# Sixteen instead of eight expert blocks between the query heads, with the low halves of their weights made on GpSimd

## The chip, the cores and the metric

The kernel runs on one core of one Trainium2 chip. The metric is the device time of one execution in microseconds (us), lower being better. The core has TensorE for matmuls, VectorE, ScalarE and GpSimd for work on tiles in SBUF, SyncE as a queue that starts transfers, and 16 DMA engines. The profile calls the engines PE, DVE, ACT, POOL and SP; PEld is TensorE's loading of weights.

## The reference

Two layers act on 512 tokens of width 1024. Each has a mixer (a gated linear recurrence in layer 0, attention in layer 1) and then a feed-forward part with 16384 experts, of which each token uses 16 in each of 8 heads. The change lies in that second part:

```python
def retrieve_chunk(xc):
    q = (xc @ q_w).reshape(TOKEN_CHUNK, PEER_HEADS, 2, PEER_HALF)
    s1 = jnp.einsum('thd,hnd->thn', q[:, :, 0], subkey1)
    s2 = jnp.einsum('thd,hnd->thn', q[:, :, 1], subkey2)
    v1, i1 = lax.top_k(s1, PEER_TOPK)
    v2, i2 = lax.top_k(s2, PEER_TOPK)
    cand = (v1[..., :, None] + v2[..., None, :]).reshape(...)
    top_s, top_c = lax.top_k(cand, PEER_TOPK)
    e1 = jnp.take_along_axis(i1, top_c // PEER_TOPK, axis=-1)
    e2 = jnp.take_along_axis(i2, top_c % PEER_TOPK, axis=-1)
    expert = e1 * PEER_KEYS + e2
    g = jax.nn.softmax(top_s, axis=-1)
    u = jnp.take(expert_u, expert, axis=0)
    act = jax.nn.gelu(jnp.einsum('thkd,td->thk', u, xc))
    w = g * act
    return jnp.einsum('thk,thkd->td', w, jnp.take(expert_v, expert, axis=0))
```

## The kernel before

Three of the four tiles of 128 tokens (384 tokens) are computed densely: each of 128 blocks of 128 experts is projected for all of them (the matrix `expert_u`), the result goes through the GELU, is multiplied by a gate that is zero where the expert wasn't chosen, and is multiplied by the block of `expert_v`. The fourth tile is gathered: GpSimd fetches the chosen rows of `expert_u` and `expert_v` by indirect transfers (L700), 128 of each, and VectorE reduces them (L706, L716).

A product of two float32 numbers is made of three matmuls. `split` (L189) has ScalarE copy a tile to a shorter format, the high half (`whi`), and VectorE subtract that from the tile, the low half (`wlo`, L192). All weights pass through one `Stream`, in the order of a plan written out by hand: `fill` (L129) loads a pair of blocks with SyncE into `wraw` (two buffers) and splits each block into `whi` and `wlo` (four buffers each), and `take` (L144) keeps three blocks ahead.

The expert part of a layer has three stages. In the query stage `queries` (L530) goes over 8 heads: two projections of queries of 512 columns (`proj_t`, L254, or `proj_early`, L235, for the first), the split of each query into `qh` and `ql`, scores against 128 keys in `sps` (L545 to L547), and the 16 best of each token by VectorE (`top16`, L521). After every second head (`ups_after`, L485), `first_up` (L554) projects two blocks of experts ahead, eight in all (`NEARLY`), and puts their activations into DRAM (`ascr`, L558). In the routing stage 48 more blocks are projected ahead (up to `NFIRST`, 56), and beside each of them a `Background` runs as much of the routes and gates as the credit `GP` pays. In the value stage (from `expert_in`, L745) the 72 blocks that were not projected ahead come first, each projected on the spot (L751); then the 56 whose activations are loaded again (L753). TensorE multiplies each by its block of `expert_v` (18 matmuls of 512 columns, L769). Beside each block `pump` pays credit for the gathered tile: 4.6 for the first eight blocks, then `PUMP[0]`, 3.7, and `PUMP[1]`, 1.4, for those from DRAM; one row costs 1.2 (fetch and reduction), and the route of the tile 18.5 in all. When the gathered tile is done, credit that is left pays for nothing, or, in layer 0, for some of the next mixer's modulation (`after`).

The code is recorded and then ordered for each engine by a scheduler, so that an engine's queue need not follow the text; in each queue instructions run in order. GpSimd's queue held, around this stage, four small operations of the norm, 48 memsets for the routes' tables (L566 to L568), and the row fetches of the value stage.

Of the kernel before, what the change touches and what calls it, by code (L numbers as in the profile page):

```python
# [26 lines left out]
PH = 8  # L27
# [3 lines left out]
ROWO = [sum(ROWN[:i]) for i in range(TOPK)]  # L31
NCAND = sum(ROWN)
NEG = -3.0e38
NFIRST = 56
NEARLY = 8
PUMP = (3.7, 1.4)
GP = 4.0
GSCALE = 32768.0
M0 = 12
# [10 lines left out]
def pool(tc, **kw):  # L50
    return tc.tile_pool(reuse_waits="tile", **kw)
# [67 lines left out]
class Stream:  # L119
# [3 lines left out]
    def __init__(self, g, items, ahead=3):  # L123
        self.g, self.ahead = g, ahead
        self.blocks = [(i, b) for i in items for b in range(i[2])]
        self.raw, self.parts = None, []
        self.n = 0

    def fill(self, last):  # L129

        g, nc = self.g, self.g.nc
        last = min(last, len(self.blocks) - 1)
        while len(self.parts) <= last:
            (src, shape, n), b = self.blocks[len(self.parts)]
            if b == 0:
                self.raw = g.wraw.tile([128, n, *shape], F32, name="wraw", tag="wraw")
                nc.sync.dma_start(self.raw, src)
            raw = self.raw[:, b]
            hi = g.wsp.tile([128, *shape], F32R, name="whi", tag="whi")
            lo = g.wsp.tile([128, *shape], F32R, name="wlo", tag="wlo")  # L140
            split(g, hi, lo, raw)
            self.parts.append((hi, lo))

    def take(self, ahead=None):  # L144
# [42 lines left out]
        g.nc.scalar.activation(out[:, half * 512:(half + 1) * 512], ps, AF.Copy)  # L187


def split(g, hi, lo, raw):  # L190
    g.nc.scalar.activation(hi, raw, AF.Copy)  # L191
    g.nc.vector.tensor_sub(lo, raw, hi)  # L192


def norm(g, cols, ng, mod=None):
# [41 lines left out]
def proj_early(g, psum, h, m):  # L237

    nc = g.nc
    w = [g.stream.take(0) for _ in range(m)]  # L240
    hhi, hlo = h
    ps = [psum.tile([128, S], F32, name="pacc", tag="acc") for _ in range(m)]
    for s in range(KD):
        for b in range(min(s + 1, m)):
            for k in range(s + 1) if s == b else (s,):
                nc.tensor.matmul(ps[b], w[b][0][:, k, :], hhi[:, k, :], start=(k == 0), stop=False)
                nc.tensor.matmul(ps[b], w[b][0][:, k, :], hlo[:, k, :], start=False, stop=False)
                nc.tensor.matmul(ps[b], w[b][1][:, k, :], hhi[:, k, :], start=False, stop=(k == KD - 1))
    return ps


def proj_t(g, psum, h, n=S):

    nc = g.nc  # L254
    whi, wlo = g.stream.take()
    hhi, hlo = h
    ps = psum.tile([128, S], F32, name="pacc", tag="acc")[:, :n]
    for k in range(KD):
        nc.tensor.matmul(ps, whi[:, k, :], hhi[:, k, :n], start=(k == 0), stop=False)  # L259
        nc.tensor.matmul(ps, whi[:, k, :], hlo[:, k, :n], start=False, stop=False)  # L260
        nc.tensor.matmul(ps, wlo[:, k, :], hhi[:, k, :n], start=False, stop=(k == KD - 1))  # L261
    return ps
# [221 lines left out]

def ups_after(hd):  # L485

    n = 2 * NEARLY // PH
    return range(hd // 2 * n, hd // 2 * n + n) if hd % 2 else range(0)


def peer_plan(q_w, sk, uT, v):

    plan = []
    up = [(uT[c], (KD, 128), 2) for c in range(PK // 2)]
    for hd in range(PH):
        q = (q_w[hd], (KD, 128), 2)
        plan += [(sk[hd], (2, 128), 1), q] if hd else [q, (sk[hd], (2, 128), 1)]
        plan += up[ups_after(hd).start // 2:ups_after(hd).stop // 2]
    down = [(v[2 * c:2 * c + 2].rearrange("c p a b -> p c a b"), (2, 512), 2) for c in range(PK // 2)]
    n = NFIRST // 2  # L500
    plan += up[NEARLY // 2:n]
    for c in range(n, PK // 2):
        plan += [up[c], down[c]]
    return plan + down[:n]


def peer(g, h, u, v, grow_fn, after, nd):


    tc, nc = g.tc, g.nc  # L510
# [3 lines left out]
    gscr = g.dram.tile([NB, 128, 128, 16], F32, name="gscr", tag="gscr")  # L514
    ascr = g.dram.tile([NFIRST, 128, ND], F32, name="ascr", tag="ascr")
    with pool(tc, name="pk", bufs=1) as pk:
# [5 lines left out]
        def top16(val, idx, src, n):  # L522
            tk = pk.tile([128, 128], F32, name="tk", tag="tk", bufs=4)
            V.max(val[:, 0:8], src)
            V.max_index(idx[:, 0:8], val[:, 0:8], src)
            V.match_replace(tk[:, :n], val[:, 0:8], src, NEG)
            V.max(val[:, 8:16], tk[:, :n])
            V.max_index(idx[:, 8:16], val[:, 8:16], tk[:, :n])

        def queries(pw, psum):  # L530

            early = []
            for hd in range(PH):
                if hd == 0:
                    early = proj_early(g, psum, h, 2)
                skh, skl = g.stream.take()
                for w in range(2):
                    ps = early.pop(0) if early else proj_t(g, psum, h)
                    qh = pw.tile([128, S], F32R, name="qh", tag="qh")
                    ql = pw.tile([128, S], F32R, name="ql", tag="ql")  # L540
                    split(g, qh, ql, ps)
                    sps = psum.tile([128, TC, 128], F32, name="sps", tag="sps", bufs=4)
                    for t in range(TC):
                        ts = slice(t * 128, (t + 1) * 128)
                        T.matmul(sps[:, t, :], qh[:, ts], skh[:, w, :], start=True, stop=False)  # L545
                        T.matmul(sps[:, t, :], qh[:, ts], skl[:, w, :], start=False, stop=False)
                        T.matmul(sps[:, t, :], ql[:, ts], skh[:, w, :], start=False, stop=True)  # L547
                    for t in range(TC):
                        top16(vals[w][:, t, hd, :], idxs[w][:, t, hd, :], sps[:, t, :], 128)
                for c in ups_after(hd):  # L550
                    first_up(pw, psum, c)

        def first_up(pw, psum, c):

            ps = proj_t(g, psum, h, ND)
            at = pw.tile([128, ND], F32, name="at", tag="at")
            A.activation(at, ps, AF.Gelu)
            nc.scalar.dma_start(ascr[c], at)  # L558
# [168 lines left out]
        with pool(tc, name="pu", bufs=1) as pu, pool(tc, name="pw", bufs=2) as pw, \  # L727
# [4 lines left out]
            bg = Background(*[route(t) for t in range(nd)], *[dense_gates(t, pu, pw, psum) for t in range(nd)])  # L732
            for c in range(NEARLY, NFIRST):
                first_up(pw, psum, c)
                bg.pump(GP)
            bg.finish()
        with pool(tc, name="vw", bufs=2) as vw, pool(tc, name="vps", bufs=1, space=PSUM) as psum:
# [4 lines left out]
            acc = [[psum.tile([128, 512], F32, name=f"vacc{t}{d}") for d in range(2)] for t in range(nd)]  # L742
            order = [*range(NFIRST, PK), *range(NFIRST)]
            ready = {}

            def expert_in(i):

                c = order[i]
                at = vw.tile([128, ND], F32, name="at2", tag="at2", bufs=3)
                if c >= NFIRST:  # L750
                    A.activation(at, proj_t(g, psum, h, ND), AF.Gelu)  # L751
# [20 lines left out]
            def pump(i):  # L772
                bg.pump(4.6 if i < 8 else PUMP[0] if order[i] >= NFIRST else PUMP[1])

# [386 lines left out]
```

## Time and profile before

| | us |
|---|---|
| runs timed | 3399.68, 3401.50, 3401.56 (median 3401.5) |
| profiled execution | 3391.94 |
| its span, from first to last instruction | 3390.2 |
| TensorE, VectorE, ScalarE, GpSimd busy | 3158.9, 2647.0, 1482.6, 790.7 |
| mean granted clock of TensorE | 0.973 |

The stages are cut from the timeline. In layer 0 the query stage runs from 314 us (the first projection) to 465 us (the last score), the routing stage to 751 us, the first part of the value stage to 1380 us and the rest to about 1648 us, where the gathered rows end at about 1578 us. In layer 1 the cuts are at 2040, 2199, 2485, 3112 and 3385 us. In the tables of windows each engine's busy time stands with the number of instructions in brackets, and a matmul's time reaches from its start to its modelled end, so that neighbouring matmuls overlap; the step from one start to the next tells more.

### The profile page before, as it was taken

Reading aid. Unit: us, or ns where it says so; the run is one execution under the profiler, and the core shown is the slowest. Engines: PE = TensorE matmul, PEld = TensorE weight load, DVE = VectorE, ACT = ScalarE, POOL = GpSimd, SP = SyncE. Lnnn points to the kernel's source line nnn. Section 1 sums busy time; section 2 is a strip of 40 time slices with the busy share of each in tenths; the row PEclk is TensorE's granted clock in tenths of the full one; section 3 lists DMA queues with packets and bytes.
Section 4 is the critical chain, followed back from the end, with each engine's and each line's share of the span. In section 5 each row is a group of like instructions: output and inputs, shape, how many; then the busy total and the mean of one; then the engine's idle time right before and its main releaser. Section 6 shows DMA issues by size and latency. Waiting matters only on the chain.

```text
span 3390.2 us, 44187 instructions
## 1 busy us (share of the span) xinstructions
PE 3158.9 (93%) x16256; PEld 2712.4 (80%) x16256; DVE 2647.0 (78%) x5245; ACT 1482.6 (44%) x2065; POOL 790.7 (23%) x672
## 2 busy tenths in 40 slices
PE   5987999999999999999999989999999999999999
PEld 4875889988888888777777767889988888887777
DVE  7867889876777787877679777799867777788775
ACT  4872237863333333333458723257843333332332
POOL 0000000003544454441000000000025454444430
PEclk9998999999999999999999989999999999999999
DMA  6445235778888889988441152336879888899994
GB/s 255 149 146 178 103 126 197 257 273 288 315 299 315 322 322 329 351 310 324 141 153 58 49 192 92 114 133 245 283 250 323 320 302 314 321 330 331 325 335 169
DMA packets 300762, 816.91 MB, mean 241 GB/s; under 512 B 24320, under 2 KB 153344, under 8 KB 272000
## 3 DMA queue, kind: packets, MB, share of 16 engines
q1 hardware_dynamic: 197312, 453.85, 38.6%
q0 software_dynamic: 75008, 269.00, 21.8%
q10 hardware_dynamic: 28224, 91.24, 6.9%
q8 instruction: 127, 2.08, 0.2%
q14 instruction: 91, 0.75, 0.1%
HBM read 733.00 MB, written 81.00 MB: 240 GB/s over the span
## 4 chain that ended last, share of the span: by engine, by line
issue 23%; PE 23%; DVE 19%; DMA 17%; POOL 10%; ACT 7%; SPq 0%; ACTq 0%; POOLq 0%; DVEq 0%
POOL rows L700 10%; DMA at<-ascr 6%; DMA rows<-in_l_v_dram,ei 6%; PE pacc L259 4%; DVE wlo L192 4%; PE pacc L260 4%; PE pacc L261 4%; PE vacc L769 2%; DVE accg L716 2%; PE gps L683 2%; DMA mw<-in_l_ffn_mw_dram 2%; DMA mw<-in_l_mix_mw_dram 1%; DVE mw L160 1%; ACT st L685 1%; ACT whi L191 1%
## 5 line engine op out<-in xcount | busy, mean ns | idle before, releaser
L191 ACT ACTIVATE whi<-wraw 128x1024 fp32r<-128x1024 f32 (+2 forms) x646 | 663.1, 1035 | 740.2 <-PE pacc L260 314.4
L261 PE MATMUL pacc<-hhi,wlo 128*128 128x384 f32 (+1 forms) x2632 | 935.4, 355 | 39.9 <-DVE wlo L192 39.9
L259 PE MATMUL pacc<-hhi,whi 128*128 128x384 f32 (+1 forms) x2632 | 930.6, 354 | 15.9 <-ACT at L751 14.4
L260 PE MATMUL pacc<-hlo,whi 128*128 128x384 f32 (+1 forms) x2632 | 930.0, 353 | 0.0
L192 DVE TENSOR_TENSOR wlo<-wraw,whi 128x1024 fp32r<-128x1024 f32 (+2 forms) x646 | 767.7, 1194 | 171.8 <-ACT whi L191 169.5
L769 PE MATMUL vacc<-whi,wh 128*128 128x512 f32 x1536 | 613.8, 400 | 23.6 <-ACT wh L191 23.4
L700 POOL DMA_INDIRECT rows<-in_l_u_dram,ei x256 | 370.1, 1446 | 1127.5 <-DMA wraw<-in_l_uT_dram 716.7
L769 PE MATMUL vacc<-wlo,wh 128*128 128x512 f32 x1536 | 612.9, 399 | 20.7 <-DVE wlo L192 20.5
L769 PE MATMUL vacc<-whi,wl 128*128 128x512 f32 x1536 | 612.1, 399 | 5.7 <-DVE wl L192 5.5
L261 PEld LDWEIGHTS pacc<-hhi,wlo 128*128 128x128 f32 x2632 | 502.7, 191 | 71.2 <-DVE wlo L192 49.8
L259 PEld LDWEIGHTS pacc<-hhi,whi 128*128 128x128 f32 x2632 | 503.1, 191 | 49.4 <-ACT at L751 16.6
L260 PEld LDWEIGHTS pacc<-hlo,whi 128*128 128x128 f32 x2632 | 502.2, 191 | 29.2 <-issue 2.4
L191 ACT ACTIVATE wh<-at 128x384 fp32r<-128x384 f32 x256 | 133.8, 524 | 806.4 <-DVE at L757 789.3
L700 POOL DMA_INDIRECT rows<-in_l_v_dram,ei x256 | 377.2, 1474 | 454.6 <-DVE accg L716 396.9
L706 DVE SCALAR_TENSOR_TENSOR rows<-rows,hn 128x1024 f32<-128x1024 f32 x256 | 304.6, 1221 | 130.3 <-DMA rows<-in_l_u_dram,ei 130.1
L769 PEld LDWEIGHTS vacc<-wlo,wh 128*128 128x128 f32 x1536 | 290.4, 189 | 94.6 <-DVE wlo L192 30.9
L769 PEld LDWEIGHTS vacc<-whi,wh 128*128 128x128 f32 x1536 | 290.7, 189 | 93.7 <-ACT wh L191 30.9
L769 PEld LDWEIGHTS vacc<-whi,wl 128*128 128x128 f32 x1536 | 290.7, 189 | 85.3 <-DVE wl L192 16.3
L716 DVE SCALAR_TENSOR_TENSOR accg<-rows,act,accg 128x1024 f32<-128x1024 f32 x254 | 325.5, 1282 | 41.0 <-DMA rows<-in_l_v_dram,ei 38.4
L757 DVE TENSOR_TENSOR at<-at,gtile 128x384 f32<-128x384 f32 x256 | 140.6, 553 | 108.4 <-DMA at<-ascr 105.9
L685 ACT ACTIVATE st<-gps 128x512 f32<-128x512 f32 x192 | 185.3, 1117 | 47.6 <-PE gps L683 45.2
L192 DVE TENSOR_TENSOR wl<-at,wh 128x384 fp32r<-128x384 f32 x256 | 141.3, 554 | 68.8 <-ACT wh L191 68.8
(266 smaller groups left out, 3229.5 us busy)
## 6 DMA issues: line engine op xcount, KB each, us to landing
wraw<-in_l_uT_dram SPq DMA_DIRECT2D x128, 1024.0 KB, 6.4
wraw<-in_l_v_dram SPq DMA_DIRECT2D x128, 1024.0 KB, 8.4
gscr<-st ACTq DMA_DIRECT2D x48, 1024.0 KB, 5.6
gtile<-gscr SPq DMA_DIRECT2D x32, 1536.0 KB, 12.3
mw<-in_l_mix_mw_dram SPq DMA_DIRECT2D x48, 512.0 KB, 6.4
mw<-in_l_ffn_mw_dram SPq DMA_DIRECT2D x48, 512.0 KB, 4.0
ascr<-at ACTq DMA_DIRECT2D x112, 192.0 KB, 4.1
at<-ascr SPq DMA_DIRECT2D x112, 192.0 KB, 5.2
```

The costliest lines, as they stand in the source:

```text
L191: g.nc.scalar.activation(hi, raw, AF.Copy)
L192: g.nc.vector.tensor_sub(lo, raw, hi)
L259: nc.tensor.matmul(ps, whi[:, k, :], hhi[:, k, :n], start=(k == 0), stop=False)
L260: nc.tensor.matmul(ps, whi[:, k, :], hlo[:, k, :n], start=False, stop=False)
L261: nc.tensor.matmul(ps, wlo[:, k, :], hhi[:, k, :n], start=False, stop=(k == KD - 1))
L683: T.matmul(gps[:, r, :], p2[:, tk_, :, :].rearrange("p a b -> p (a b)"), pg[i][:, :, tk_, :], start=(i == 0), stop=(i == 1))
L685: A.activation(st[:, :, q * 4:q * 4 + 4].rearrange("p e t -> p t e"), gps, AF.Copy, scale=1.0 / GSCALE)
L700: nc.gpsimd.indirect_dma_start(out=rows, out_offset=None, in_=src, in_offset=bass.IndirectOffsetOnAxis(ap=ei[:, j:j + 1], axis=0))
L706: V.scalar_tensor_tensor(r, r, 1.0, hn, op0=OP.mult, op1=OP.mult, accum_out=act[:, j:j + 1]))
L716: tc.keep_in_program_order(V.scalar_tensor_tensor(acc, r, w, acc, op0=OP.mult, op1=OP.add))
L757: V.tensor_tensor(at.rearrange("p (b t) -> p b t", t=16), at.rearrange("p (b t) -> p b t", t=16), env["gt"][:, :, c % 8, :], op=OP.mult)
L769: T.matmul(acc[t][d], x[:, ts], y[:, d, :], start=(i == 0 and x is wh and y is vh), stop=(i == PK - 1 and x is wl))
```

## The change

`NEARLY` goes from 8 to 16 and `NFIRST` from 56 to 64, so the routing stage still has 48 blocks and the value stage projects 64 on the spot and loads 64. `ups_after` gives two blocks after each head. While `queries` is recorded, the stream's subtractions go to GpSimd. `PUMP[1]` goes from 1.4 to 1.55.

```diff
-NFIRST = 56
-NEARLY = 8
-PUMP = (3.7, 1.4)
+NFIRST = 64
+NEARLY = 16
+PUMP = (3.7, 1.55)
...
+        self.on_pool = False
...
-            split(g, hi, lo, raw)
+            split(g, hi, lo, raw, nc.gpsimd if self.on_pool else nc.vector)
...
-def split(g, hi, lo, raw):
+def split(g, hi, lo, raw, eng=None):
     g.nc.scalar.activation(hi, raw, AF.Copy)
-    g.nc.vector.tensor_sub(lo, raw, hi)
+    (eng or g.nc.vector).tensor_sub(lo, raw, hi)
...
 def ups_after(hd):
-    n = 2 * NEARLY // PH
-    return range(hd // 2 * n, hd // 2 * n + n) if hd % 2 else range(0)
+    n = NEARLY // PH
+    return range(hd * n, hd * n + n)
...
             early = []
+            g.stream.on_pool = True
             for hd in range(PH):
...
                     first_up(pw, psum, c)
+            g.stream.on_pool = False
```

GpSimd's queue in layer 0, from the last memsets of the tables (`thr`, `rowlen`, `col`) to the row fetches, before:

```order
55 L566 MEMSET thr 128x64
56 L567 MEMSET rowlen 128x64
57 L568 MEMSET col 128x64
58 L94 IOTA ji 128x128
59 L700 DMA rows<-in_l_u_dram,ei 128x1024 x128
60 L700 DMA rows<-in_l_v_dram,ei 128x1024 x128
```

In the changed kernel the low halves of the weights follow the memsets (the narrow ones are those of the keys):

```order
58 L570 MEMSET rowlen 128x64
59 L571 MEMSET col 128x64
60 L193 TENSOR_TENSOR wlo<-wraw,whi 128x1024
61 L193 TENSOR_TENSOR wlo<-wraw,whi 128x256
62 L193 TENSOR_TENSOR wlo<-wraw,whi 128x1024 x4
```

That pattern of four wide and one narrow goes on for the heads, 33 wide and 7 narrow low halves in a layer, and the row fetches stand behind all of them.

VectorE's queue in the query stage, around one `ql` (the low half of a query), with the searches for the 16 best before and behind it, before:

```order
456 L528 MAX_INDEX idxs_2501<-vals_2499,tk 128x8
457 L526 MATCH_REPLACE tk<-vals_2499,sps 128x128
458 L192 TENSOR_TENSOR wlo<-wraw,whi 128x1024
459 L527 MAX vals_2499<-tk 128x8
460 L192 TENSOR_TENSOR wlo<-wraw,whi 128x1024
461 L528 MAX_INDEX idxs_2501<-vals_2499,tk 128x8
462 L192 TENSOR_TENSOR wlo<-wraw,whi 128x256
463 L192 TENSOR_TENSOR ql<-pacc,qh 128x512
464 L192 TENSOR_TENSOR wlo<-wraw,whi 128x1024
465 L524 MAX vals_2498<-sps 128x8
```

The same place in the changed kernel:

```order
494 L527 MATCH_REPLACE tk<-vals_2499,sps 128x128
495 L528 MAX vals_2499<-tk 128x8
496 L529 MAX_INDEX idxs_2501<-vals_2499,tk 128x8
497 L193 TENSOR_TENSOR ql<-pacc,qh 128x512
498 L525 MAX vals_2498<-sps 128x8
```

No low half of a weight stands between the searches and `ql` any more.

ScalarE's queue over a head and more in the query stage: `whi` are the high halves of weights, `qh` those of queries, `at` the activations of an expert block and `ascr` their way to DRAM. Before, the two blocks stand together after a pair of heads:

```order
268 L191 ACTIVATE whi<-wraw 128x256
269 L191 ACTIVATE qh<-pacc 128x512
270 L191 ACTIVATE whi<-wraw 128x1024
271 L557 ACTIVATE at<-pacc 128x384
272 L558 DMA ascr<-at 128x384
273 L191 ACTIVATE whi<-wraw 128x1024
274 L191 ACTIVATE whi<-wraw 128x256
275 L557 ACTIVATE at<-pacc 128x384
276 L558 DMA ascr<-at 128x384
277 L191 ACTIVATE qh<-pacc 128x512
```

In the changed kernel there are two of them for each head:

```order
257 L192 ACTIVATE whi<-wraw 128x256
258 L192 ACTIVATE qh<-pacc 128x512
259 L192 ACTIVATE whi<-wraw 128x1024 x2
260 L560 ACTIVATE at<-pacc 128x384
261 L561 DMA ascr<-at 128x384
262 L192 ACTIVATE whi<-wraw 128x1024
263 L560 ACTIVATE at<-pacc 128x384
264 L561 DMA ascr<-at 128x384
265 L192 ACTIVATE whi<-wraw 128x1024
266 L192 ACTIVATE qh<-pacc 128x512
```

A `whi` stands ahead of each `qh` there, as it mostly did before.

## Rows read from the trace of the kernel before

**Rows 1.** The page: busy us of each engine over the span.

```profile
PE 3158.9 (93%) x16256; PEld 2712.4 (80%) x16256; DVE 2647.0 (78%) x5245; ACT 1482.6 (44%) x2065; POOL 790.7 (23%) x672
```

**Rows 2.** Windows: length, busy PE, PEld, DVE, ACT, POOL; PEclk, DMA share, GB/s.

```profile
314.00:465.00 151.00, 145.46 (x752) 122.34 (x753) 121.57 (x549) 45.90 (x62) 4.22 (x48) 1.00 0.25 91
465.00:751.00 286.00, 271.12 (x2028) 259.92 (x2028) 255.60 (x655) 202.02 (x243) 0.24 (x1) 0.98 0.65 227
755.00:1380.00 625.00, 599.33 (x2927) 533.23 (x2926) 476.49 (x616) 202.64 (x279) 301.96 (x209) 0.98 0.86 310
1380.00:1580.00 200.00, 186.37 (x766) 144.99 (x765) 156.47 (x196) 63.67 (x86) 73.11 (x47) 0.97 0.94 340
2040.00:2199.00 159.00, 151.92 (x752) 128.39 (x753) 122.96 (x553) 45.47 (x61) 4.45 (x49) 0.94 0.25 88
...
3112.00:3315.00 203.00, 185.43 (x762) 144.99 (x761) 153.03 (x181) 63.33 (x86) 73.76 (x48) 0.97 0.92 330
```

**Rows 3.** Timeline of TensorE, 380 to 384.6 us: start, us, line, operation.

```profile
380.02 0.28 PE L545 MATMUL sps<-whi,qh 128*128 128x128 f32 x1
...
380.91 0.28 PE L547 MATMUL sps<-whi,ql 128*128 128x128 f32 x1
...
381.31 0.40 PE L259 MATMUL pacc<-hhi,whi 128*128 128x512 f32 x1
...
382.00 0.33 PE L259 MATMUL pacc<-hhi,whi 128*128 128x384 f32 x1
...
383.43 0.33 PE L259 MATMUL pacc<-hhi,whi 128*128 128x384 f32 x1
...
384.48 0.33 PE L259 MATMUL pacc<-hhi,whi 128*128 128x384 f32 x1
```

**Rows 4.** Groups by form, 314 to 465 us: count, busy us, mean ns, idle before.

```profile
L192 DVE TENSOR_TENSOR wlo<-wraw,whi 128x1024 fp32r<-128x1024 f32 x24 | 29.1, 1214 | 8.8 <-ACT whi L191 7.3 <-PE sps L547 1.4
```

**Rows 5.** Waits, 314 to 465 us: us in total, times, longest.

```profile
PEld sps L547 <- DVE ql L192: 8.1, 13, 1.5
...
PE sps L547 <- DVE ql L192: 3.3, 4, 1.1
PEld sps L545 <- ACT qh L191: 2.7, 12, 0.2
```

**Rows 6.** Groups of GpSimd by form over the span.

```profile
L214 POOL TENSOR_TENSOR rs<-ms,mhalf 128x1 f32<-128x1 f32 x16 | 13.5, 843 | 512.5 <-DVE ms L212 507.2 <-DVE col_l_mix L161 4.4 <-DVE acol L225 0.9
...
L481 POOL IOTA iota_f<- 128x128 f16 x2 | 0.8, 380 | 5.0 <-PE xt L217 5.0
```

**Rows 7.** Windows of the instructions on the value accumulators alone (PE, PEld, DVE, ACT).

```profile
1580.00:1648.00 68.00, 65.18 (x276) 50.98 (x274) 3.45 (x5) 0.00 (x0) 1.00 0.68 240
```

**Rows 8.** Waits, 1380 to 1580 us.

```profile
ACT whi L191 <- DMA wraw<-in_l_v_dram: 45.2, 11, 8.4
...
PEld vacc L769 <- DVE wlo L192: 12.6, 11, 2.1
PE vacc L769 <- DVE wlo L192: 8.0, 8, 1.6
```

**Rows 9.** The page's DMA issues: count, KB each, us to landing.

```profile
wraw<-in_l_v_dram SPq DMA_DIRECT2D x128, 1024.0 KB, 8.4
...
gtile<-gscr SPq DMA_DIRECT2D x32, 1536.0 KB, 12.3
...
at<-ascr SPq DMA_DIRECT2D x112, 192.0 KB, 5.2
```

**Rows 10.** The page's DMA queues: GpSimd's own (packets, MB, share).

```profile
q0 software_dynamic: 75008, 269.00, 21.8%
```

## The prediction

> **What bounds the kernel now.** The page's busy line comes first: TensorE is busy for 93% of the span and VectorE for 78% [rows 1]. A share over the whole span says little of two stages that differ, so the windows by stage come next [rows 2]. In one layer the query stage lasts 151 us (159 us in the second layer), the routing stage 286 us, and the value stage some 890 us: a first part of 625 us in which each expert is projected on the spot, a second part in which the activations come back from DRAM, with fetches of expert rows beside them for 200 us (203 us in the second layer), and a tail without fetches. TensorE is the busiest engine in each of them, but its busy times overlap, so the third view is the timeline, for the step from one matmul to the next when nothing is waited for: 0.89 us over 8 steps, or 0.111 us, for 128 columns; 0.69 over 3, or 0.23 us, for 512; 1.05 over 6, or 0.175 us, for 384 [rows 3]. I call the sum of these steps TensorE's work.
>
> The query stage has 752 matmuls: 16 projections of 24 at 512 columns (384), 192 for scores at 128, and 176 at 384 columns, which is a little over seven expert blocks. The work is 384 x 0.23 + 192 x 0.111 + 176 x 0.175 = 140.4 us of 151, so 10.6 us are idle; the same count in 159 us leaves 18.6 us, there with a granted clock of 0.94 of full speed instead of 1.00 [rows 2]. An expert of the first value part is 24 x 0.175 + 18 x 0.23 = 8.34 us of work; 2927 matmuls at 42 each are 69.7 experts in 625 us, 8.97 us each, so work fills 93%. In the second part 766 matmuls at 18 each are 42.6 experts in 200 us, 4.70 us each (762 in 203 us: 4.80), for 4.14 us of work, with the DMA engines at 0.94 and 0.92 [rows 2]; in the tail 276 matmuls are 15.3 experts in 68 us, 4.43 us each [rows 7]. So TensorE paces all the stages that the change touches. An expert block costs the same 24 matmuls wherever it is projected, and the change can win or lose only by the idle time at the two places.
>
> **The change part by part.** It has four parts, each taken for one layer.
>
> Eight more expert blocks stand in the query stage. They add 8 x 24 x 0.175 = +33.6 us of work to a stage in which TensorE has 10.6 us to spare. The low halves leave VectorE: 24 of them at 1.214 us each now run there in that window [rows 4], 29 of its 121.6 busy us. What TensorE waits for is, in the main, the low half of the queries, ql, behind other work of VectorE (8.1 and 3.3 us, as its weight loads and its matmuls see the same stalls), and the high half, qh (2.7 us) [rows 5]. In the new order ql still stands behind the top-16 of the half before and qh behind a whi on ScalarE, so I let the stalls be what they are: 0, with bounds of -10.6 (all gone) and +10.6 (doubled).
>
> GpSimd makes the low halves. No row shows this operation there. One tensor operation of one column takes 0.84 us on it and an iota of 128 columns 0.38 us [rows 6]; eight iotas, or 3.0 us, is the upper end for 1024 columns, and VectorE's 1.214 us [rows 4] the lower. I take 2.4 us, nearer to the row that is GpSimd's own. A head needs four wide ones and one narrow, at most 4.25 x 3.0 = 12.9 us, while TensorE needs 48 x 0.23 + 24 x 0.111 + 48 x 0.175 = 22.1 us for it; the four buffers of high and low halves keep blocks three ahead. So it is hidden, by either end. What is queued behind each low half on GpSimd is the next low half alone, since its row fetches begin only in the value stage. At the start it isn't hidden fully: the fifth block's low half stands behind 48 memsets, SyncE's next load of queries reuses that block's buffer, and the first queries wait behind two more high halves on ScalarE. I take +1 us, between 0 and +6. (The Trainium skill, "GPSIMD Engine Reference", section 3.1, gives 4497 ns for a tensor_tensor of 2048 columns; half of it, an estimate of 2.25 us, would leave the sum as it is.)
>
> The routing stage keeps its 48 blocks and its credit. Three of them come with low halves that GpSimd made: 3 x 1.214 = 3.6 us less on a VectorE that is busy for 255.6 of 286 us [rows 2, 4]. TensorE is busy for 271.1 there and may gain nothing by it, so between 0 and -3.6; I take -2.5 us. (The Trainium skill, "GPSIMD Engine Reference", section 8, says that GpSimd shares its SBUF interfaces with VectorE and contends with its instructions that have two SBUF inputs, which the routes' tensor operations are. No run here shows it. By that rule this gain goes and the sum is 2.5 us a layer higher.)
>
> The value stage has 64 experts projected on the spot instead of 72, and 64 from DRAM instead of 56. The first part loses 8 x 8.97 = -71.8 us. The second part gains eight experts, and more of it is spent at the slower pace: the pumps must pay 325.7 credits for the gathered tokens (18.5 for the route, 256 fetches at 1.2). Before, the first part paid 8 x 4.6 + 64 x 3.7 = 273.6, so 52.1 were left, 37 experts at 1.4; now it pays 8 x 4.6 + 56 x 3.7 = 244.0 and 81.7 are left, 53 experts at 1.55. Experts without a fetch beside them fall from 19 to 11. So 16 x 4.75 (mean of the two layers) - 8 x 4.43 = +40.6 us, if the pace of each kind stays. It may not: an expert there moves half of 1024 KB of values, 192 KB of activations and an eighth of 1536 KB of gates [rows 9], 0.92 MB together, and 1.4/1.2 fetches of 269/512 = 0.525 MB [rows 10], in all 1.53 MB; at 1.55 it is 1.60 MB, 4.3% more, on engines that are 0.94 busy. If transfers set the pace, that is 53 x 4.75 x 0.043 = +10.8 us; if TensorE's wait for VectorE does, 0. ScalarE waits for the loads of values for 45.2 us there, but TensorE's own waits are mostly for VectorE's wlo, 12.6 and 8.0 us [rows 8]. I take +4. The value stage is then -71.8 + 40.6 + 4 = -27.2 us, between -31.2 and -20.4.
>
> The sum of a layer: 33.6 + 0 + 1 - 2.5 - 27.2 = +4.9 us, and +9.8 us for two. The profiled execution takes 3391.94 us (3390.2 of span and 1.7 around it), so 3401.7; the median of the runs shown is 3401.5, 9.6 us above that execution, and on its scale the forecast is 3411 us. All lower ends together give 33.6 - 10.6 + 0 - 3.6 - 31.2 = -11.8 a layer, 3378 us; all upper ends 33.6 + 10.6 + 6 + 0 - 20.4 = +29.8, 3461 us.
>
> **The rivals.** The first ends faster: the query stage takes the blocks in its idle time. Its mechanism is VectorE: relieved of 29 us of low halves, it makes every ql before TensorE comes to it, and the 10.6 us of idle (18.6 in the second layer) go. For it speaks that the named waits are VectorE's [rows 5]; against it, that the top-16 alone stands between two ql in the new order, and that part of the second layer's idle time goes with a lower clock. It decides from some 6 us of idle saved a layer; at its full price, 3411 - 10.6 - 18.6 - 2 = 3380 us.
>
> The second is no change: the extra fetches are hidden behind TensorE (-4 a layer) and nothing else moves, 3411 - 8 = 3403 us. For it speaks that VectorE, at 156 of 200 us, has room for them [rows 2].
>
> The third is that transfers set the pace of the second value part: -20.4 instead of -27.2 a layer, 3411 + 14 = 3425 us. For it speaks the DMA share of 0.94; against it, that TensorE does 88% of that part in work. (The Trainium skill, "Trainium Kernel Development and Optimization", section Key Constraints, says that all queues run on the same 16 DMA engines and interleave; by that rule GpSimd's extra fetches delay SyncE's loads of values, and the wait of 45.2 us for those is what the trace has to say for it.)
>
> The fourth is that GpSimd can't keep up: above 22.1 / 4.25 = 5.2 us for a wide low half it sets the pace of the heads. At 6 us that is 3.4 us for each of 16 heads, +54, 3465 us. The row of the iota speaks against it. That the change doesn't do what it says is excluded by the order: 33 wide low halves stand on GpSimd in each layer, and two blocks after each head.
>
> **How the numbers follow.** The forecast has a chance of 0.38, the query stage's idle time 0.20, no change 0.20, transfers 0.15, a slow GpSimd 0.07. The forecast's own range is 3403 to 3419. Some 0.2%, 6.8 us, is what a measurement can tell from no change, so no change lies from 3394.7 to 3408.3. Faster is the first rival and a little of the second, where stalls shrink as well: 0.27. Within 0.2% are the rest of the second and the lower third of the forecast's range: 0.27. Slower is what remains, 0.46. The range of 3380 to 3438 leaves out the slow GpSimd and the outer halves of the first and third rivals.
>
> **What would show it.** In the changed profile the stretch from the first projection to the last score should be some 34 us longer in each layer, with about 370 matmuls at 384 columns and still some 11 us idle; if it is less than 26 us longer, the first rival is at work. The low half on GpSimd should take 2 to 3 us and release few waits of TensorE. The first value part should be 72 us shorter at an unchanged 9 us an expert. The second part and tail should be some 45 us longer, at 4.7 to 4.9 us an expert while fetches last; at 4.95 or more it is the transfers. The forecast is wrong if the query stage grows much less than its added work, or if the gathered rows end so late that the last tile waits for them.

## The result, and the profile after

The changed kernel takes 3445.7 us (median of four runs, 3438.5 to 3448.0) where the kernel before takes 3401.5 (four runs, 3399.7 to 3410.0): 1.012 times as long, 95% interval 1.010 to 1.014, or some 44 us slower. The forecast was 3411 us with a range that ended at 3438, so the time is outside the range, on the side that the forecast had called likelier. The profiled execution has a span of 3446.2 us and takes 3448.0; against the profiled execution of before, 3391.9, that is 56 us. The profiled execution of before is 9.6 us under its median and that of the change 2.2 us over it, so the stages below show some 12 us more loss than the medians do.

The page's busy line of the changed kernel, to be read against [rows 1]:

```profile
PE 3174.2 (92%) x16256; PEld 2727.6 (79%) x16256; DVE 2579.3 (75%) x5165; ACT 1482.8 (43%) x2065; POOL 968.3 (28%) x752
```

TensorE has the same 16256 matmuls, VectorE has given up 80 low halves and GpSimd has them. Nothing here explains 44 us. The windows by stage do (columns as in [rows 2]): query, routing, first value part, part with fetches, tail, then the query stage and the part with fetches of the second layer, and last the whole value stage of the first layer.

```profile
314.00:493.00 179.00, 176.88 (x928) 153.53 (x927) 97.50 (x523) 56.23 (x78) 81.31 (x86) 1.00 0.33 115
493.00:781.00 288.00, 273.06 (x2049) 262.96 (x2047) 255.93 (x651) 201.06 (x245) 5.16 (x3) 0.98 0.63 225
781.00:1345.00 564.00, 532.64 (x2606) 475.58 (x2606) 422.17 (x564) 181.44 (x249) 264.39 (x183) 0.98 0.85 305
1345.00:1629.00 284.00, 253.19 (x1024) 197.67 (x1022) 213.99 (x255) 85.59 (x116) 112.45 (x73) 0.95 0.91 324
1629.00:1680.00 51.00, 43.18 (x159) 32.63 (x160) 36.73 (x72) 15.35 (x21) 1.12 (x2) 0.90 0.70 256
2072.00:2253.00 181.00, 177.93 (x922) 154.44 (x923) 98.08 (x524) 55.59 (x76) 81.33 (x86) 0.98 0.32 113
3105.00:3396.00 291.00, 253.47 (x1016) 197.28 (x1016) 212.11 (x248) 84.30 (x115) 112.11 (x73) 0.95 0.88 312
781.00:1680.00 899.00, 829.00 (x3787) 705.88 (x3787) 672.89 (x887) 282.38 (x384) 377.95 (x258) 0.97 0.86 308
```

The same window over the value stage of the kernel before:

```profile
751.00:1647.00 896.00, 854.39 (x3983) 732.46 (x3982) 683.92 (x897) 292.07 (x400) 376.36 (x258) 0.98 0.86 312
```

Against the last row above: the changed value stage has 196 matmuls fewer (8 x 24, and a few at the cut) and lasts as long. DMA share and GB/s are nearly the same too. With the stages cut at single events of the timeline (first projection, last score, first matmul on the value accumulators, last activation made on the spot, last use of a fetched row, last value matmul), in us:

| stage | before, layer 1 | after, layer 1 | before, layer 2 | after, layer 2 | change forecast |
|---|---|---|---|---|---|
| query | 150.5 | 178.3 | 158.7 | 181.5 | +34.6 |
| routing | 286.8 | 288.6 | 286.6 | 289.5 | -2.5 |
| value, first part | 629.0 | 563.9 | 627.3 | 562.2 | -71.8 |
| value, with fetches, and tail | 195.8 + 70.9 | 283.9 + 51.4 | 201.0 + 70.5 | 290.9 + 44.4 | +44.6 |
| value, whole | 895.6 | 899.2 | 898.8 | 897.5 | -27.2 |

The added work of the query stage is paid (+28 and +23 us), and the value stage gives nothing back (+4 and -1). Its length varies by some 10 us from one execution to the next: with the split of before, the run with GpSimd alone and the run with 40 blocks in the routing stage, both described below, took 898.1 and 908.4, and 898.7 and 904.0 us in the two layers. That is well under the 27.2 us that failed to come. What TensorE waits for in the part with fetches stands in the waits of the changed kernel, 1350 to 1690 us (the view of [rows 8], over a longer stretch):

```profile
POOL rows L703 <- DVE accg L719: 153.8, 51, 9.8
...
ACT whi L192 <- DMA wraw<-in_l_v_dram: 75.7, 19, 8.4
...
DVE at L760 <- DMA at<-ascr: 68.1, 32, 6.6
PEld vacc L772 <- DVE wlo L193: 27.4, 16, 6.6
...
PE vacc L772 <- DVE wlo L193: 20.8, 12, 6.1
PEld vacc L772 <- DVE wl L193: 12.4, 6, 4.8
```

TensorE's waits are all for an engine, none for a DMA, and that is how the kernel before looked as well. But behind these engines stand two waits for loads: ScalarE's for the values (75.7 us) and VectorE's for the activations (68.1 us). TensorE's longest wait shows how the second is coupled to it. TensorE's timeline there (start, us, line, operation, idle before):

```profile
1472.64 0.39 PE L772 MATMUL vacc<-whi,wh 128*128 128x512 f32 x1
1479.15 0.79 PE L772 MATMUL vacc<-wlo,wh 128*128 128x512 f32 x1 [6.12 <-DVE wlo L193]
...
1481.02 0.63 PE L772 MATMUL vacc<-whi,wl 128*128 128x512 f32 x1
1481.45 0.63 PE L772 MATMUL vacc<-whi,wh 128*128 128x512 f32 x1
```

And VectorE's:

```profile
1467.01 2.60 DVE L719 SCALAR_TENSOR_TENSOR accg<-rows,act,accg 128x1024 f32<-128x1024 f32 x2
1476.21 0.56 DVE L760 TENSOR_TENSOR at<-at,gtile 128x384 f32<-128x384 f32 x1 [6.60 <-DMA at<-ascr]
1476.69 1.28 DVE L719 SCALAR_TENSOR_TENSOR accg<-rows,act,accg 128x1024 f32<-128x1024 f32 x1
1477.88 1.22 DVE L193 TENSOR_TENSOR wlo<-wraw,whi 128x1024 fp32r<-128x1024 f32 x1
```

The product of an activation with its gates (L760) waits 6.6 us for its load; the low half for which TensorE waits stands two instructions behind it, and so the stall is booked to VectorE. VectorE works in order, and so a late load stops it: it is TensorE's releaser and was itself released by a transfer. After the stall the matmuls follow each other at 0.43 us (1481.02, 1481.45) in place of the 0.23 us of [rows 3]: the lower of the clock's two levels, 1.2 GHz (the granted clock from 1479.0 to 1482.0 us is 0.50). The granted clock of this part is 0.95, and 0.90 in the tail, where it was 0.97 [rows 2] and 1.00 [rows 7].

### The profile page after: what moved, and what is told of

It is laid out like the page before. It is cut to its first block, busy times and chain, and to the rows that moved or that the text cites. A ratio compares the mean times of both kernels' runs of the same rounds, so it can differ in the third digit from the quotient of the medians.

```text
span 3446.2 us, 44333 instructions
## 1 busy us (share of the span) xinstructions
PE 3174.2 (92%) x16256; PEld 2727.6 (79%) x16256; DVE 2579.3 (75%) x5165; ACT 1482.8 (43%) x2065; POOL 968.3 (28%) x752
## 4 chain that ended last, share of the span: by engine, by line
PE 29%; issue 24%; DMA 16%; DVE 15%; POOL 10%; ACT 6%; SPq 0%; POOLq 0%; DVEq 0%; ACTq 0%
POOL rows L703 10%; PE pacc L260 6%; PE pacc L261 6%; PE pacc L262 6%; DMA at<-ascr 5%; DMA rows<-in_l_v_dram,ei 4%; DVE wlo L193 4%; PE vacc L772 3%; DVE accg L719 2%; PE gps L686 2%; ACT st L688 2%; DMA mw<-in_l_ffn_mw_dram 1%; DMA mw<-in_l_mix_mw_dram 1%; DVE mw L161 1%; ACT whi L192 1%
## 5 line engine op out<-in xcount | busy, mean ns | idle before, releaser
L193 DVE TENSOR_TENSOR wlo<-wraw,whi 128x1024 fp32r<-128x1024 f32 (+1 forms) x566 | 682.0, 1210 | 159.7 <-ACT whi L192 158.8
L772 PE MATMUL vacc<-wlo,wh 128*128 128x512 f32 x1536 | 620.4, 404 | 50.3 <-DVE wlo L193 50.1
L760 DVE TENSOR_TENSOR at<-at,gtile 128x384 f32<-128x384 f32 x256 | 140.5, 554 | 148.3 <-DMA at<-ascr 147.4
L193 POOL TENSOR_TENSOR wlo<-wraw,whi 128x1024 fp32r<-128x1024 f32 (+1 forms) x80 | 168.2, 2106 | 187.7 <-ACT whi L192 187.7
L688 ACT ACTIVATE st<-gps 128x512 f32<-128x512 f32 x192 | 183.7, 1120 | 53.2 <-PE gps L686 44.4
```

Of the source, the lines that this page charges most:

```text
L193: (eng or g.nc.vector).tensor_sub(lo, raw, hi)
L688: A.activation(st[:, :, q * 4:q * 4 + 4].rearrange("p e t -> p t e"), gps, AF.Copy, scale=1.0 / GSCALE)
L760: V.tensor_tensor(at.rearrange("p (b t) -> p b t", t=16), at.rearrange("p (b t) -> p b t", t=16), env["gt"][:, :, c % 8, :], op=OP.mult)
L772: T.matmul(acc[t][d], x[:, ts], y[:, d, :], start=(i == 0 and x is wh and y is vh), stop=(i == PK - 1 and x is wl))
```

## The experiments

Two theories stood at the start. **V**: TensorE's work left the value stage, but the transfers of fetched rows set its length, so the work that was taken away only turned into idle time. **P**: the work on GpSimd is what costs (its low halves are late, or it holds something up).

**GpSimd alone.** The kernel before, with the low halves of the query stage on GpSimd and nothing else.

```diff
 (in the changed kernel)
-NFIRST = 64; NEARLY = 16; PUMP = (3.7, 1.55)
+NFIRST = 56; NEARLY = 8;  PUMP = (3.7, 1.4)
 (ups_after as before)
```

> The kernel before (8 blocks between the heads, 56 ahead, pump 1.4) with the low halves of the query stage on GpSimd and nothing else changed. Theory V (the change's loss lies in the value stage, which is as long as its transfers and fetches make it and gives nothing back for 8 blocks less on TensorE): the query stages lose a little of their idle time, 3401 us less 5 to 20, so 3382 to 3397. Theory P (GpSimd's low halves cost time, by latency or by slowing VectorE): 3410 us or more.

3406.7 us against 3402.0: ratio 1.002, 1.000 to 1.005. Neither expectation held: not the loss of P (3410 us or more), and no gain. Its query stage:

```profile
315.00:464.00 149.00, 143.29 (x735) 119.48 (x734) 96.97 (x523) 45.37 (x62) 63.63 (x78) 1.00 0.26 92
```

VectorE falls from 121.6 us [rows 2] to 97.0, and the stage, by the cut of the table, from 150.5 to 148.5 (in the second layer from 158.7 to 153.1). VectorE wasn't its limit.

**The blocks alone.** The changed kernel, with its low halves on VectorE again.

```diff
-            g.stream.on_pool = True
+            g.stream.on_pool = False
```

> The changed kernel with all low halves on VectorE again: only the blocks move. Theory V: the value stages stay as long as in the changed kernel (some 898 us each) and the query stages lose what GpSimd gave, so 3446 us or up to 30 more. Theory P: the time falls clearly under 3446 us, to 3425 or less.

3439.3 us, 1.011 (1.009 to 1.014). The loss is there without GpSimd's part; theory P falls as its cause. GpSimd's part may cost some 5 us: this run is 6 us below the changed kernel, and GpSimd alone was 5 us above the kernel before. The query stage and the value stage of this run:

```profile
780.00:1676.00 896.00, 831.13 (x3788) 707.54 (x3786) 673.38 (x888) 281.95 (x383) 375.85 (x258) 0.97 0.86 309
315.00:494.00 179.00, 177.12 (x934) 153.56 (x935) 129.81 (x560) 55.84 (x77) 4.26 (x49) 1.00 0.33 115
```

**Half of each fetched row**, in the kernel before and in the changed one. A fetch brings 512 of the 1024 columns, and VectorE reads these twice, so that its work stays; the other half of each row is left out. The table is taken as rows of 512 for that, so the half rows come from its first half, and the first product goes to a spare tile instead of back into the row.

```diff
-nc.gpsimd.indirect_dma_start(out=rows, out_offset=None, in_=src,
+nc.gpsimd.indirect_dma_start(out=rows[:, 0:512], out_offset=None, in_=src,
 ...
-V.scalar_tensor_tensor(acc, r, w, acc, ...)
+V.scalar_tensor_tensor(two(acc), twice(r), w, two(acc), ...)
```

> The kernel before, with half of each fetched expert row left out: an indirect transfer brings 512 of 1024 columns and VectorE reads them twice, so its instructions keep their size. 67 MB a layer less are moved in the value stage of some 275 MB. If transfers set the pace of that stage (theory V), it falls from 896 us to its work on TensorE and VectorE, some 830 to 860 us, so 3330 to 3380 us in all. If TensorE and VectorE pace it, 3390 us or more.

> The changed kernel with the same half rows. If transfers ate the 33 us of work that TensorE saves in a value stage (theory V), they come back here: the value stage is some 25 to 33 us shorter than that of the half rows before, and the whole is within 10 us of it. If the loss has another cause (the order of VectorE's queue, latency of each fetch, the clock), this stays 30 to 50 us above the half rows before, as with whole rows.

3253.5 us from before (0.956, 0.953 to 0.958) and 3287.5 from the changed kernel (0.966, 0.963 to 0.969). First the value stage from before, then that of the changed one:

```profile
752.00:1582.00 830.00, 829.42 (x3979) 723.64 (x3977) 687.64 (x896) 298.54 (x398) 377.67 (x258) 1.00 0.74 255
```

```profile
784.00:1601.00 817.00, 801.95 (x3788) 691.53 (x3788) 676.49 (x888) 287.14 (x383) 384.75 (x258) 1.00 0.75 257
```

Fewer bytes, in as many fetches, make the value stage of before 66 us shorter, to 830, with TensorE busy for 829.4 of it. That is its real floor: 72 x 8.34 + 56 x 4.14 = 832 us, by the work per expert that the prediction had worked out. V had said 830 to 860 there; its total of 3330 to 3380 us was too high, since the gain comes in both layers. The changed kernel comes to 817 and 811 in the two layers, of a floor of 64 x 8.34 + 64 x 4.14 = 799; so 13 and 20 us of the 34 come back. V had said that the two kernels would end within 10 us of each other, and they end 34 apart. So V is half answered. Taken by itself, the changed kernel gets 82 and 87 us of its value stages back by half the bytes, with GpSimd's 258 operations there unchanged, so it is not their issuing that costs the time. Its first part, its part with fetches and its tail in the first layer:

```profile
784.00:1304.00 520.00, 520.00 (x2606) 469.01 (x2607) 429.41 (x566) 185.75 (x249) 269.09 (x185) 1.00 0.71 242
1304.00:1550.00 246.00, 240.64 (x1026) 191.57 (x1025) 210.93 (x252) 85.41 (x115) 114.53 (x72) 1.00 0.84 290
1550.00:1601.00 51.00, 41.31 (x159) 30.95 (x158) 36.15 (x72) 15.98 (x21) 1.12 (x2) 0.93 0.68 250
```

In the first part TensorE is never idle any more; of the 15 us of idle time left, 5 lie in the part with fetches and 10 in the tail, which has none.

**One fetch for 128**, again in both. The first fetch of each run is made and the other 127 are not; VectorE reads the same rows each time, so its work stays and 127 of 128 fetches are left out, with their transfers, their issuing on GpSimd and VectorE's waits for them. Here too the product goes to a spare tile.

```diff
-                r = fetch(u, j)
+                r = fetch(u, j) if j == 0 else r
 ...
-                r = fetch(v, j)
+                r = fetch(v, j) if j == 0 else r
```

> The kernel before with one fetch of expert rows in place of each run of 128: VectorE's reductions stay, 254 of 256 transfers of 0.52 MB a layer are left out. With half rows the value stage fell from 896 to 830 us, where TensorE had 15 us idle. If TensorE paces it then, 825 to 830 us, so 3240 to 3255 us in all; if transfers still did, 790 us or less.

> The changed kernel with the same one fetch. If fetches' transfers are the whole cause of the loss, the value stage is 33 us shorter than that of the one-fetch kernel before (8 blocks less on TensorE), and the whole differs from it by the query and routing stages' 28 to 33 us less those 33: within 5 us a layer, so within 10 us of it. If reductions on VectorE near the end hold up the tail, or loads of activations hold up TensorE, it stays 15 to 35 us above.

3258.3 us from before (0.958, 0.956 to 0.960), 3252.3 from the changed kernel (0.956, 0.955 to 0.958): 6 us apart, where the expectation had within 10 if the fetches are the whole cause. The value stages, of before and then of the changed one:

```profile
752.00:1582.00 830.00, 829.52 (x3981) 724.12 (x3980) 688.63 (x896) 297.20 (x400) 4.12 (x4) 1.00 0.52 176
```

```profile
785.00:1583.00 798.00, 796.38 (x3790) 690.85 (x3789) 677.58 (x889) 285.15 (x383) 4.12 (x4) 1.00 0.53 180
```

Without the fetches the value stage shrinks by 32 us, as the 8 x 24 x 0.175 = 33.6 us of TensorE's work say. The order, the buffers, VectorE's reductions and the loads of weights are all still there: it is the fetches that take the gain away. The landings show one way. This is the list of DMA issues of the changed kernel with one fetch (KB each, median us from issue to landing):

```profile
wraw<-in_l_v_dram SPq DMA_DIRECT2D x128, 1024.0 KB, 4.9
...
gtile<-gscr SPq DMA_DIRECT2D x32, 1536.0 KB, 9.1
...
at<-ascr SPq DMA_DIRECT2D x128, 192.0 KB, 3.7
```

And of the changed kernel itself:

```profile
wraw<-in_l_v_dram SPq DMA_DIRECT2D x128, 1024.0 KB, 8.4
...
gtile<-gscr SPq DMA_DIRECT2D x32, 1536.0 KB, 12.8
...
at<-ascr SPq DMA_DIRECT2D x128, 192.0 KB, 5.5
```

Loads that SyncE issues land 3.5, 3.7 and 1.8 us later because GpSimd's fetches run beside them. (The Trainium skill, "Trainium Kernel Development and Optimization", section Key Constraints, says that all queues run on the same 16 DMA engines and interleave; these landings agree.) In the kernel before, the loads land nearly as late: 8.4, 12.3 and 5.2 us [rows 9].

There is a second way. VectorE waits for the fetched rows themselves, and the low halves for TensorE stand behind these waits as well. VectorE's waits for rows in the first part of the changed kernel (781 to 1345 us), and in the whole value stage of its run with half rows (784 to 1601 us):

```profile
DVE rows L709 <- DMA rows<-in_l_u_dram,ei: 64.4, 27, 4.3
```

```profile
DVE junk L717 <- DMA rows<-in_l_u_dram,ei: 4.6, 3, 3.4
```

**More of the fetches in the first part.** The changed kernel with a higher payment for an expert that is projected on the spot, so that the second part again has 1.4.

```diff
-PUMP = (3.7, 1.55)
+PUMP = (4.22, 1.4)
```

> The changed kernel with PUMP (4.22, 1.4): the first part pays for as many fetches as before the change (272 credits), at 3.52 instead of 3.08 an expert, and the part with loaded activations again has 38 experts with fetches and 26 without. If only the place of the fetches were at fault, the second part and tail fall from 335 us to some 295 and the first part stays near 563: 3446 - 80 = 3370 us. If transfers pace the first part as well, it gets some 35 us longer and the whole stays within 15 us of 3446.

3463.5 us, 1.018 (1.016 to 1.020), 18 above the changed kernel. Its first part, the part with fetches and the tail:

```profile
784.00:1378.00 594.00, 546.67 (x2612) 481.79 (x2611) 450.35 (x588) 181.57 (x249) 277.21 (x207) 0.96 0.86 309
1378.00:1586.00 208.00, 185.22 (x750) 143.72 (x748) 153.22 (x189) 61.46 (x84) 71.88 (x50) 0.96 0.90 328
1586.00:1692.00 106.00, 102.45 (x430) 80.10 (x431) 69.44 (x113) 38.69 (x52) 1.12 (x2) 1.00 0.68 233
```

Theory V had said within 15 us of the changed kernel, which is just missed, and the other 3370, which is far off. The first part becomes 30 us longer, with the same matmuls and 24 fetches more: it pays for fetches as the second does. The place of the fetches isn't at fault. The tail, with few of them, runs at full clock.

**More buffers for the activations.** Five instead of three, in the changed kernel and in the one before, so that their loads start earlier.

```diff
-at = vw.tile([128, ND], F32, name="at2", tag="at2", bufs=3)
+at = vw.tile([128, ND], F32, name="at2", tag="at2", bufs=5)
```

> The changed kernel with five instead of three buffers for an expert's activations (at2). SyncE's queue holds a load of activations until one is free, 133 us of waits for VectorE's wl in the second part, and the loads of values stand behind it. If that order costs TensorE its stalls of 3 to 6 us, the second part and tail fall by 20 us or more a layer: 3400 us or less. If transfers are late by their volume, within 10 us of 3446.

> The kernel before with five instead of three buffers for an expert's activations. On the changed kernel they gave 21 us in all, 17 to 19 us in each value stage. If they give loads a longer start wherever transfers pace the stage, they give 10 to 20 us a layer here too: 3360 to 3385 us. If they only help the changed kernel's longer part with loaded activations, within 5 us of 3401.

The changed kernel comes to 3424.9 us (1.008, 1.006 to 1.009), 21 below itself and between the two expectations; the one before to 3407.3 (1.001, 0.999 to 1.003), no gain. The value stage of the changed one, then of the other:

```profile
783.00:1665.00 882.00, 825.20 (x3786) 703.25 (x3786) 672.28 (x887) 279.32 (x383) 378.33 (x258) 0.97 0.87 314
```

```profile
754.00:1659.00 905.00, 859.85 (x3981) 738.24 (x3979) 684.57 (x896) 290.11 (x399) 373.15 (x258) 0.97 0.85 308
```

So a part of the loss goes with these buffers, as the wait of VectorE for a late activation in the timeline suggests: 17 and 19 us in the value stages of the two profiled executions, but only some 10 a layer by the medians, since the one profiled with five buffers is the fastest of its four. In its first layer VectorE still waits 55.8 us for activations, in place of 68.1. Why the kernel before doesn't gain by them stays open.

**The gain given to the routing stage.** Sixteen blocks between the heads as in the change, but 56 ahead in all, so that eight leave the routing stage and not the value stage.

```diff
-NFIRST = 64; PUMP = (3.7, 1.55); GP = 4.0
+NFIRST = 56; PUMP = (3.7, 1.4);  GP = 4.8
```

> The changed kernel with 56 blocks ahead and pump 1.4 as before the change, so 16 between the heads and 40 in the routing stage (credit 4.8 there). The value stage is that of the kernel before: 896 us expected. The query stage should be 28 us a layer longer, the routing stage shorter by as much of its 8 x 4.2 = 33 us as TensorE, and not VectorE with 255 busy of 286 us, paces it. If TensorE does: 3401 us less 0 to 10; if VectorE does: 3420 to 3455 us.

3422.0 us, 1.006 (1.003 to 1.008), at the lower end of what was expected if VectorE paces the routing stage. Its routing stage:

```profile
498.00:766.00 268.00, 247.50 (x1854) 234.50 (x1854) 247.78 (x644) 189.43 (x227) 5.10 (x3) 0.95 0.61 222
```

With 33.6 us less for TensorE to do than in the changed kernel it is only 20 us shorter, 268.4 by the cut. VectorE is busy for 247.8 of them, which would fit VectorE as the limit but doesn't show it. The query stage pays its 30 us here too (180.7 against 150.5). There is no stage here that gives a block back at its full price.

**The change turned round.** No blocks between the heads and 48 ahead in all, with the low halves of the query stage on GpSimd; then the same with five buffers.

```diff
-NFIRST = 64; NEARLY = 16; PUMP = (3.7, 1.55)
+NFIRST = 48; NEARLY = 0;  PUMP = (3.4, 1.4)
```

> The change turned round: low halves of the query stage on GpSimd, no block between the heads and 48 in the routing stage, so 80 projected on the spot (pump 3.4, 1.4). Theory T (transfers set the length of the value stage, some 897 us, until TensorE's work reaches it; that work was some 815 us before and is 33 us more here): the value stage stays within 15 us of 897 and the query stage loses 25 to 30 us, so 3401 - 2 x (28 - 0 to 15), 3345 to 3375 us. If TensorE paces the value stage, it gets 36 us longer and the whole is 3400 to 3420 us.

> The same as e11_n48_q0 with five buffers for an expert's activations. Theory T: another 10 to 20 us less a layer than that one only as far as TensorE's work allows; 3325 to 3365 us. If buffers help only where activations are loaded, less than 8 us, since 48 instead of 64 are.

3397.2 us (0.998, 0.996 to 1.000) and 3396.0 (0.996, 0.994 to 0.998): the second is faster than the kernel before by 0.4%. The query stage and the value stage of the first:

```profile
315.00:452.00 137.00, 125.27 (x582) 100.08 (x583) 97.28 (x521) 35.50 (x49) 48.91 (x71) 0.93 0.22 75
736.00:1647.00 911.00, 877.62 (x4172) 760.19 (x4170) 694.24 (x905) 303.49 (x415) 387.77 (x258) 0.99 0.86 309
```

The value stage takes eight more blocks, 33.6 us of work, for 15 and 12 us in the two layers, since they fill time in which TensorE waited for transfers; the query stage gives back only 13 and 11 of the 33.6 and lies idle for 28 and 38 us. That is why turning the change round gains so little. Theory T (3345 to 3375 us) was right on the value stage, 911 and 910 us where it had said within 15 of 897, and wrong on the query stage, from which it expected 25 to 30 us. The five buffers took 1 us, so they help little here.

## Why the prediction was wrong

**The step that failed** is "So TensorE paces all the stages that the change touches", and with it the term of -27.2 us for the value stage, which measured +3.6 and -1.3. The prediction had worked out 8.34 us of work for 8.97 us of time for an expert of the first part, and 4.14 for 4.70 to 4.80 in the second, and took the rest for a share that goes along with the work. It is not: it is time in which fetches hold up the engines. The run with one fetch shows 830 us of value stage before and 798 after, just the work; the fetches add 66 us to the one and 101 to the other, and so both end near 897. In the first layer every split with full fetches, those with five buffers included, took between 883 and 915 us for that stage, whether TensorE's work was 799, 832 or 866 us (64, 72 or 80 experts on the spot). The bytes are nearly the same in all of them, 280 MB before (896 x 312), 277 after and 281 in the turned kernel.

By terms, for the first layer: the first part lost 65.1 us instead of 71.8 (2606 matmuls at 42 each are 62 experts, 9.09 us each, not 8.97). The part with fetches and the tail gained 68.6 instead of 44.6: 1024 matmuls at 18 each are 56.9 experts in 284 us, 4.99 each, over the 4.95 that the prediction had named as the sign of transfers; and the 8.8 experts of the tail took 5.8 us each in place of 4.43, at a granted clock of 0.90.

**The third rival had the mechanism and a price too low.** It was put at +6.8 us a layer, from 4.3% more bytes per expert in the second part alone. The runs put the fetches at the whole 31 and 26 us that failed to come, because the first part pays for them as well, as the earlier fetches and the half rows showed. The wait of 45.2 us for the loads of values [rows 8] is ScalarE's; the row that the stall of 6.1 us leads to stands in the same view of the kernel before, and the prediction passed over it:

```profile
DVE at L757 <- DMA at<-ascr: 30.8, 18, 6.0
```

What the prediction set against this rival, that TensorE's own waits name VectorE, fell: in order, VectorE passes a transfer's lateness on under its own name.

**The direction** came from the query stage and was right. Its growth was forecast at 33.6 + 1 us and measured 27.8 and 22.8. By the prediction's own count, 928 matmuls are 384 x 0.23 + 192 x 0.111 + 352 x 0.175 = 171.2 us of 179, so 7.8 us lie idle where 10.6 did; in the second layer 922 matmuls, or 170.2 us of 181, leave 10.8 of 18.6. So the first rival, that the blocks take idle time, holds for 3 and 8 us, and in the second layer by the prediction's own sign of less than 26 us. The prediction took 0 there. The rival's mechanism, VectorE relieved, isn't what did it: with the low halves back on VectorE the stage takes 178.1 and 178.3 us, no longer than in the changed kernel.

**GpSimd** was taken at 2.4 us for a wide low half, a choice between 1.2 and 3.0 without a row of that operation:

```profile
L193 POOL TENSOR_TENSOR wlo<-wraw,whi 128x1024 fp32r<-128x1024 f32 x66 | 157.9, 2396 | 137.3 <-ACT whi L192 137.3
```

It measured 2.396 us, closer than the choice deserved, and all of GpSimd's idle time before it is a wait for the high half, so it kept up; the fourth rival is out. (The Trainium skill, "GPSIMD Engine Reference", section 3.1, led to an estimate of 2.25 us; the trace has 6% more.) In the query stage TensorE's waits for VectorE's ql shrank but did not go: [rows 5] had 8.1 and 3.3 us, and the changed kernel, 314 to 493 us, has

```profile
DVE ql L193 <- ACT qh L192: 63.2, 8, 8.8
...
PEld sps L549 <- DVE ql L193: 5.8, 14, 2.3
...
PEld sps L547 <- ACT qh L192: 4.1, 15, 0.3
...
PE sps L549 <- DVE ql L193: 2.0, 1, 2.0
```

VectorE now waits for ScalarE's high half for 63.2 us and has time to spare; it was the pace of nothing there. **The routing stage** was to gain 2.5 us by three low halves less and lost 1.8 and 2.9, with VectorE as busy as before (255.9 us to 255.6). With the low halves on VectorE it takes 286.2 and 286.1 us, so the loss of 2 to 3 us goes with GpSimd's part; how is not shown.

**What stays open.** The fetches are shown to be the cause, and their bytes to be most of it. How much of it is the DMA engines' capacity, and how much the lateness of single loads that an engine working in order passes on, is not: half the bytes brought back 13 to 20 us of the difference a layer and two more buffers 10 to 19, but both together were not run. The timelines allow two estimates. In the value stage of before TensorE idles for 42 and 47 us (first and second layer), in that of the change for 70 and 70. Followed back from each releaser to the first transfer, 9 and 14 us of this ended at a load of activations before the change and 26 and 32 after it, while the part that ended at fetched rows went only from 22 and 25 to 25 and 29: most of the growth is activations that come late. Matmuls at the clock's lower level, counted by steps of 1.6 to 2.3 times those of [rows 3], cost 12 and 11 us beyond their higher-level steps before, and 21 and 18 after, so the clock is some 7 to 9 us of the loss a layer.

## What to carry to other kernels

Work out an engine's floor for a stage (count times step) and don't scale the gap between floor and time with the work: it may belong to something else and need not shrink when the engine gets less to do. Here a gap of 7% was the fetches, and work moved out of that stage came back as idle time while the stage that received it paid for most of it. Where a matmul waits for an engine that works in order, ask what that engine waited for just before. A cheap test before such a move is to leave out the suspected transfers and see which stage falls to its floor.

## What the runs showed of the hardware

After a stall of 6.1 us the granted clock was 0.50 and the matmuls of 512 columns ran at 0.43 us each instead of 0.23; the first ten took 3.9 us instead of 2.3, so an idle time caused by transfers cost some 1.6 us more than its own length. With full fetches the value stage, taken whole, had a DMA share of 0.85 to 0.87 and at most 314 GB/s in the first layer of each kernel, although a stretch of it reached 340 [rows 2]. At that share, well below 1, the stage's length no longer followed TensorE's work; that the share itself is the limit isn't shown. And an operation moved from VectorE (1.214 us) to GpSimd (2.396 us) doubled in duration and moved the whole time by no more than 5 to 6 us (3406.7 against 3402.0 us, 3445.7 against 3439.3), since neither of them set the pace of the query stage.
